# Exchanging the fourth sum over a and the fourth sum over b in the small round of a two-matmul kernel with GELU

## The chip, the cores and the metric

The kernel runs on one core of a Trainium2 chip. The metric is the device time of one execution in microseconds (us), and the time given for a kernel is the median of several runs. TensorE (PE in the profile; its weight loads are PEld) does the matrix products and writes them to PSUM, in eight banks of 128 x 512 fp32. VectorE (DVE) and ScalarE (ACT) read PSUM and the on-chip memory SBUF. GpSimd (POOL) and SyncE (SP) issue transfers here. Each engine works through its own list of instructions in the order in which the program gives them, and engines wait for each other by semaphores.

## The reference

```python
# a: 1024 x 1024, b: 1024 x 2048, c: 2048 x 1024, all float32
def reference(a, b, c):
    h = np.matmul(a, b)
    h = 0.5 * h * (1 + np.tanh(np.sqrt(2 / np.pi) * (h + 0.044715 * h ** 3)))
    return np.matmul(h, c).astype(np.float32)
```

Two matrix products with a GELU between them.

## The kernel before

The kernel holds the first product transposed: sixteen tiles of 128 columns of b, each against the 1024 rows of a, in two halves of 512. Tiles 0 to 3 are computed in the plain way while a and b are still coming in. Tiles 4 to 7 are the *small round*, tiles 8 to 15 the *large round*, and the product with c is a third one. Each round splits both of its operands into quarters and computes seven products of quarters where the plain way has eight; for this it needs sums and differences of quarters, which VectorE forms in SBUF. The sums over b are called s1 to s4 (`A` holds the quarters of b), the sums over a are t1 to t4 (`B` holds those of a).

```python
class Seven:
    def dve(self, dst, x, y, op, n=1, part=None):      # one sum, in n instructions
        w = self.kt // n
        for i in range(n) if part is None else (part,):
            r = slice(i * w, (i + 1) * w)
            nc.vector.tensor_tensor(out=dst[:, r], in0=x[:, r], in1=y[:, r], op=op)
    # ... cut: t1, t2, t3, s1, s2
    def t4(self, dst, n=1):
        self.last_t = dst
        self.dve(dst, self.t[1], self.B[1][0], SUB, n)
    def s3(self, n=1, part=None):
        self.dve(self.s[2], self.A[0][0], self.A[1][0], SUB, n, part)
    def s4(self, dst, n=1):
        self.last_s = dst
        self.dve(dst, self.A[0][1], self.s[1], SUB, n)
    # ... cut: plain_t, plain_s (copies on ScalarE)
    def product(self, p, l, r, j, start, c0=0, w=H):   # kt matmuls into one bank
        for k in range(self.kt):
            nc.tensor.matmul(p[:, ds(c0, w)], l[:, k, ts(j, 128)], r[:, k, ds(c0, w)],
                             start=(start and k == 0), stop=(k == self.kt - 1),
                             skip_group_check=not start)

BB = [[aT[:, 0, 0:4], aT[:, 1, 0:4]], [aT[:, 0, 4:8], aT[:, 1, 4:8]]]
zero = Seven(4, quarters(b1, H, 256), BB, [None] * 4, [None] * 4, 2)   # small round, n=2
one = Seven(4, quarters(b2, 0, H), BB, [None] * 4, zero.t)             # large round, n=4
```

In the small round `kt` is 4, so a product into one bank is four matmuls, and there are two banks (`n=2`): eight matmuls for each of the seven products. t4 is made by two instructions, each for two of the four k, and s4 by one.

```python
t4, x01 = pair(0)                      # halves of SBUF tiles x0, x1, x3
zero.s = [x31[:, :, 0:256], x01[:, :, 0:256], x11[:, :, 0:256], x01[:, :, 256:]]
one.s = [x31, x01, x11, x01]

def snap(tag, p, name):                # ScalarE copies a bank to SBUF
    st = pieces(tag, 4, [128, H], F32, name)
    nc.scalar.activation(st, p, AF.Copy)
    return st

def plus(p, st):                       # VectorE adds a bank and a copy
    ot = pieces("o", 4, [128, H], F32, "ot")
    nc.vector.tensor_tensor(out=ot, in0=p, in1=st, op=ADD)
    return ot

def seven(w, done, between):           # done applies the GELU (ScalarE) in the first two rounds
    # ... cut: names of the quarters and banks
    for j in J:
        w.product(px[j], A11, B11, j, True)                 # P1
        p1[j] = snap("m", px[j], "p1")                      # (a case of the third round is cut)
    between("P1")
    for j in J:
        p = bank(P2[j])
        w.product(p, A12, B21, j, True)                     # P2
        done(0, 0, j, plus(p, p1[j]))
    between("P2")
    py = [bank(i) for i in PY]
    for j in J:
        w.product(py[j], w.s[0], w.t[0], j, True)           # P5
    between("P5")
    for j in J:
        w.product(px[j], w.s[1], w.t[1], j, False)          # P6
        v[j] = snap("v", px[j], "v")
    between("P6")
    c22 = []
    for j in J:
        w.product(px[j], w.s[2], w.t[2], j, False)          # P7
        u[j] = snap("m", px[j], "u")
        c22.append(plus(py[j], u[j]))
        between(f"P7{j}")

    def p3(first):
        for j in J:
            if first:
                done(1, 1, j, c22[j])
            w.product(py[j], w.last_s, w.t[3], j, False)    # P3 reads s4
            done(0, 1, j, plus(py[j], v[j]))
        between("P3")

    def p4(first):
        for j in J:
            if first:
                done(1, 1, j, c22[j])
            w.product(px[j], w.s[3], w.last_t, j, False)    # P4 reads t4
            done(1, 0, j, px[j])

    for i, f in enumerate((p4, p3) if w.n == 2 else (p3, p4)):
        f(i == 0)
    # ... cut: the end of the third round

def between0(n):                       # VectorE's work between the products of the small round
    if n == "P1":
        zero.plain_s()
        zero.plain_t(2, 1)
    elif n == "P2":
        zero.s3()
        zero.s4(x31[:, :, 256:])
    elif n == "P5":
        zero.t4(t4, 2)
        one.last_t = t4

zero.s1()
zero.s2()
seven(zero, done0, between0)
one.s[3] = slot("b1", [128, 2, 4, H], F32R, "x1")[:, 0]
one.s1()
one.s2()
seven(one, done1, between1)
# ... cut: the third round, the product with c, and its stores
```

In the small round (`w.n == 2`) P4 runs ahead of P3; in the others P3 runs first. The large round uses the same t1 to t4 again.

Of the kernel before, what the change touches and what calls it, by code (L numbers as in the profile page):

```python
# [19 lines left out]
def kernel(ctx, tc, a, b, c, out):  # L20
# [183 lines left out]
    def quarters(b, c0, w):  # L204
        return [[b[:, 0:4, ds(c0, w)], b[:, 4:8, ds(c0, w)]],
                [b[:, 0:4, ds(c0 + w, w)], b[:, 4:8, ds(c0 + w, w)]]]

    zero = Seven(4, quarters(b1, H, 256), BB, [None] * 4, [None] * 4, 2)
# [151 lines left out]
    def between0(n):  # L360
        if n == "P1":
            zero.plain_s()
            zero.plain_t(2, 1)
        elif n == "P2":
            zero.s3()
            zero.s4(x31[:, :, 256:])
        elif n == "P5":
            zero.t4(t4, 2)
            one.last_t = t4

    def done1(i, l, j, p):
        gelu(8 + 4 * i + j, l, p)
# [16 lines left out]
# [5 lines that stand above are left out]
# [68 lines left out]
```

## Time and profile before

| | before |
|---|---|
| time, median of 3 runs | 120.03 us (119.86 to 120.13) |
| span of the profiled execution | 118.1 us |
| small round on TensorE | 26.0 to 39.4 us |
| large round on TensorE | 39.4 to 64.5 us |
| product with c on TensorE | 64.5 to 114.8 us |
| VectorE busy between 26.0 and 39.4 us | 10.85 of 13.40 us |
| ScalarE busy there | 10.13 us |
| TensorE's granted clock | 1.00 throughout |

A profile line such as `L152 DVE TENSOR_TENSOR x<-b,x` is an instruction of line 152 of the kernel (the sums are all in the helper `dve`, line 152; `plus` is line 283, `snap` 278, the GELU 107, and the matmuls of `product` 194), with the tile it writes and those it reads. What stands in square brackets behind it is the time its engine sat idle ahead of it, and what ended this wait. A matmul's end is modelled, while its start is recorded. The chain that ended last is followed back from the last instruction of the kernel, at each step to what released it.

### The profile page before, as it was taken

The page shows a single profiled execution, that of the slowest core. Times are in us where ns is not written, and L with a number is a line of the kernel's source. Part 1 is how long each engine was busy: PE and PEld are TensorE (multiplying, and loading weights), DVE is VectorE, ACT ScalarE, POOL GpSimd, SP SyncE. Part 2 cuts the span into 40 slices and gives each one's busy share as a digit, 9 for nine tenths or more (in the row PEclk, how much of TensorE's full clock was granted, in tenths as well). Part 3 has the DMA queues.
Part 4 walks back from the last instruction along what each step waited for, and adds up shares of the span by engine and source line. Part 5 has one row for each costly group of instructions (what it writes and reads, how often), then busy time and mean ns, then how long its engine had stood idle before and what let it go on. Part 6 is the DMA issues. An engine that isn't in the chain of part 4 may idle for free.

```text
span 118.1 us, 1469 instructions
## 1 busy us (share of the span) xinstructions
PE 111.9 (95%) x535; PEld 77.1 (65%) x540; DVE 90.5 (77%) x104; ACT 58.7 (50%) x96; POOL 11.0 (9%) x21
## 2 busy tenths in 40 slices
PE   5998899999998999999999999999999999999980
PEld 5654346544866545888887444588888888888860
DVE  0243697796996899772779999999999986964670
ACT  5046756899767689246679347800042992000000
POOL 2000007952223100000000000000000000000000
PEclk9999999999999999999999999999999999999999
DMA  3999999999999999999000000061000002014993
GB/s 88 289 371 366 366 354 305 177 205 207 205 206 213 211 212 212 211 211 212 15 0 0 0 6 0 0 221 45 0 0 0 0 0 92 3 39 175 364 350 137
DMA packets 13542, 17.91 MB, mean 152 GB/s; under 512 B 736, under 2 KB 8928, under 8 KB 13536
## 3 DMA queue, kind: packets, MB, share of 16 engines
q0 software_dynamic: 5344, 7.34, 35.2%
q1 hardware_dynamic: 8192, 10.49, 26.1%
q8 instruction: 4, 0.07, 0.2%
q14 instruction: 2, 0.02, 0.0%
HBM read 20.97 MB, written 4.19 MB: 213 GB/s over the span
## 4 chain that ended last, share of the span: by engine, by line
PE 80%; DMA 8%; DVE 5%; SPq 2%; issue 1%; ACT 1%; ACTq 0%; DVEq 0%
PE ps L194 69%; PE ps L103 8%; DMA sta<-in_a_dram 8%; DVE x L152 4%; PE pt L129 2%; SPq L68 1%; DVE ot L283 1%; ACT ab L97 1%; SPq L72 1%; DVE ot L349 0%; ACTq L97 0%; DVEq L283 0%
## 5 line engine op out<-in xcount | busy, mean ns | idle before, releaser
L194 PE MATMUL ps<-x,s 128*128 128x512 f32 x128 | 29.6, 391 | 0.0
L194 PEld LDWEIGHTS ps<-x,s 128*128 128x128 f32 x128 | 24.0, 188 | 5.1
L194 PE MATMUL ps<-x,x 128*128 128x512 f32 x96 | 22.9, 394 | 0.0
L194 PEld LDWEIGHTS ps<-x,x 128*128 128x128 f32 x96 | 18.0, 188 | 3.9
L103 PE MATMUL ps<-aT,b 128*128 128x512 bf16 x62 | 15.0, 379 | 0.7 <-DVE aT L131 0.5
L278 ACT ACTIVATE v<-ps 128x512 f32<-128x512 f32 x10 | 6.0, 598 | 17.8 <-PE ps L194 17.8
L194 PE MATMUL ps<-c_sb,hT 128*128 128x512 bf16 (+1 forms) x70 | 14.1, 355 | 0.1
L194 PE MATMUL ps<-x 128*128 128x512 f32 x56 | 13.5, 395 | 0.3 <-DVE x L152 0.3
L194 PEld LDWEIGHTS ps<-x 128*128 128x128 f32 x56 | 10.2, 188 | 3.3 <-DVE x L152 0.8
L107 ACT ACTIVATE hT<-ot 128x512 bf16<-128x512 f32 x18 | 10.7, 625 | 3.3 <-DVE ot L283 3.3
L283 DVE TENSOR_TENSOR ot<-ps,v 128x512 f32<-128x512 f32 x10 | 6.7, 687 | 6.4 <-DMA out_dram<-ot 3.9
L194 PEld LDWEIGHTS <-hT 128*128 128x128 bf16 x72 | 6.9, 98 | 7.0 <-issue 0.5
L194 PE MATMUL ps<-aT,b 128*128 128x512 bf16 x47 | 10.6, 379 | 0.1
L283 DVE TENSOR_TENSOR ot<-ps,u 128x512 f32<-128x512 f32 x10 | 6.7, 689 | 5.2 <-ACT u L278 5.2
L103 PEld LDWEIGHTS <-b 128*128 128x128 bf16 x64 | 5.8, 97 | 6.8 <-DVE aT L131 1.0
L131 DVE COPY aT<-pt 128x512 bf16<-128x512 bf16 x16 | 6.0, 419 | 5.2 <-PE pt L129 5.2
L152 DVE TENSOR_TENSOR x<-c_sb 128x1024 fp32r<-128x1024 bf16 x8 | 9.2, 1216 | 0.0
L194 PEld LDWEIGHTS <-b 128*128 128x128 bf16 x48 | 4.6, 98 | 5.7 <-issue 0.3
L152 DVE TENSOR_TENSOR x<-b 128x1024 fp32r<-128x1024 bf16 (+1 forms) x4 | 7.0, 1752 | 1.0 <-DMA b<-in_b_dram 1.0
L107 ACT ACTIVATE hT<-ps 128x512 bf16<-128x512 f32 x14 | 7.3, 596 | 0.5 <-PE ps L103 0.5
L278 ACT ACTIVATE u<-ps 128x512 f32<-128x512 f32 x10 | 5.8, 596 | 3.4 <-PE ps L194 3.2
L97 ACT ACTIVATE ab<-sta 128x512 bf16<-128x512 f32 (+1 forms) x7 | 5.0, 747 | 4.9 <-DMA sta<-in_a_dram 4.9
(39 smaller groups left out, 111.8 us busy)
## 6 DMA issues: line engine op xcount, KB each, us to landing
sta<-in_a_dram SPq DMA_DIRECT2D x8, 512.0 KB, 9.1
c_sb<-in_c_dram POOLq DMA_DIRECT2D x8, 512.0 KB, 19.8
b<-in_b_dram POOLq DMA_DIRECT2D x6, 512.0 KB, 10.9
out_dram<-ot SPq DMA_DIRECT2D x12, 256.0 KB, 2.1
stb<-in_b_dram SPq DMA_DIRECT2D x4, 512.0 KB, 8.7
out_dram<-ot SPq DMA_DIRECT2D x8, 128.0 KB, 2.0
```

Of the source, the lines that this page charges most:

```text
L68: nc.sync.dma_start(out=sta[q // 2][:, h, q % 2], in_=av[:, 4 * h:4 * h + 4, ds(q * 256, 256)])
L72: nc.sync.dma_start(out=stb[:, 2 * q:2 * q + 2], in_=bv[:, 2 * q:2 * q + 2, 0:H])
L97: nc.scalar.activation(dst, src, AF.Copy)
L103: nc.tensor.matmul(p, b1[:, k, ts(t, 128)], aT[:, h, k], start=(k == 0), stop=(k == KT - 1))
L107: nc.scalar.activation(hT[h][:, t], p, AF.Gelu_apprx_tanh)
L129: nc.tensor.transpose(pt[:, n, ts(m, 128)], ab[:, m, ts(n, 128)], ident)
L131: nc.vector.tensor_copy(aT[:, h, 2 * q + n], pt[:, n])
L152: nc.vector.tensor_tensor(out=dst[:, r], in0=x[:, r], in1=y[:, r], op=op)
L194: nc.tensor.matmul(p[:, ds(c0, w)], l[:, k, ts(j, 128)], r[:, k, ds(c0, w)], start=(start and k == 0), stop=(k == self.kt - 1), skip_group ...
L278: nc.scalar.activation(st, p, AF.Copy)
L283: nc.vector.tensor_tensor(out=ot, in0=p, in1=st, op=ADD)
```

## The change

In the small round, VectorE now forms t4 (the fourth sum over a) behind s3, and s4 (the fourth sum over b) behind t4; before, s4 came first. t4 is issued ahead of the product P5, s4 behind it. The point of it is the order in which the products ask for these sums: P4 reads t4, P3 reads s4, and in this round P4 comes first.

```diff
@@ -363,10 +363,10 @@
             zero.plain_t(2, 1)
         elif n == "P2":
             zero.s3()
-            zero.s4(x31[:, :, 256:])
-        elif n == "P5":
             zero.t4(t4, 2)
             one.last_t = t4
+        elif n == "P5":
+            zero.s4(x31[:, :, 256:])
 
     def done1(i, l, j, p):
         gelu(8 + 4 * i + j, l, p)
```

## Prediction

> **What bounds the kernel now.** I read the page first, then the chain that ended last over the small round, then the timeline of each engine there, then single starts.
>
> The page's first part and the first line of its part 4:
>
> ```profile
> PE 111.9 (95%) x535; PEld 77.1 (65%) x540; DVE 90.5 (77%) x104; ACT 58.7 (50%) x96; POOL 11.0 (9%) x21
> ...
> PE 80%; DMA 8%; DVE 5%; SPq 2%; issue 1%; ACT 1%; ACTq 0%; DVEq 0%
> ```
>
> TensorE (PE) is busy 95% of a 118.1 us span and carries 80% of the chain. VectorE (DVE) carries 5%, some 5.9 us. That piece is the interesting one, because the change is on VectorE. The chain between 29 and 42 us, in columns of start, length and what:
>
> ```profile
> 30.21 1.28 DVE ot L283 x2
> 31.49 4.55 DVE x L152 x4
> 36.04 0.04 issue
> 36.09 3.71 PE ps L194 x15
> ```
>
> So VectorE holds the end of the kernel for two additions of a bank and a copy (L283) and four sums (L152: s3, s4 and the two halves of t4). At 36.09 TensorE takes over, and from there to 114.81 the whole chain is TensorE with pieces of 0.05 us between; after 39.3 us its matmuls show no wait for another engine at all. The weight loads wait there three times 0.3 us, on "issue". Whatever moves 36.09 therefore moves the end by as much, unless something else stops TensorE on the way.
>
> VectorE's own timeline, from the sum s3 on (start, length, instruction):
>
> ```profile
> 31.41 1.22 DVE L152 TENSOR_TENSOR x<-b 128x1024 fp32r<-128x1024 bf16 x1
> 32.54 1.22 DVE L152 TENSOR_TENSOR x<-b,x 128x1024 fp32r<-128x1024 bf16 x1
> 33.67 2.36 DVE L152 TENSOR_TENSOR x<-x,aT 128x1024 fp32r<-128x1024 f32 x2
> 35.95 1.28 DVE L283 TENSOR_TENSOR ot<-ps,u 128x512 f32<-128x512 f32 x2
> 38.70 0.69 DVE L283 TENSOR_TENSOR ot<-ps,v 128x512 f32<-128x512 f32 x1 [1.47 <-PE ps L194]
> 39.60 0.69 DVE L283 TENSOR_TENSOR ot<-ps,v 128x512 f32<-128x512 f32 x1 [0.21 <-PE ps L194]
> ```
>
> They are s3, s4 (it reads b), t4 in two halves (it reads aT), the two additions that take c22 out of PSUM, then those that take the outputs of P3. No gap lies between the sums: their starts are 1.13 us apart. The same stretch on the weight loads and on the matmuls:
>
> ```profile
> 35.01 0.30 PEld L194 LDWEIGHTS ps<-x 128*128 128x128 f32 x2 [0.23 <-ACT u L278]
> 36.09 3.06 PEld L194 LDWEIGHTS ps<-x 128*128 128x128 f32 x14 [0.78 <-DVE x L152]
> ...
> 36.09 3.48 PE L194 MATMUL ps<-x 128*128 128x512 f32 x14 [0.34 <-DVE x L152]
> 39.41 3.84 PE L194 MATMUL ps<-aT,b 128*128 128x512 bf16 x16
> ```
>
> P4 and P3 are eight matmuls each. Two of P4's run at 35.01, then the loads stop for 0.78 us and 14 follow. So the stop is inside P4, ahead of its third matmul, k=2, the first that reads the second half of t4. That half starts at 34.81, takes 1.22 and ends at 36.03. P4 comes first of the two products in the small round, and needs t4; s4 is needed only by P3 behind it. VectorE makes them in the opposite order.
>
> **What the Trainium skill says.** "VectorE: DVE Perf Modes", The TRN2 errata, gives (N+151)/0.96 ns for a two-tensor add in fp32: 1224 ns for N=1024. The four sums here measure 1.22 us each, whichever input is bf16, so exchanging them costs nothing by itself. "PSUM — Partial Sum Buffer", Engine vs sequencer instructions, has VectorE's queue as strictly first in, first out, and matmuls in program order. The trace agrees: the last input of t4 (t2's second half, at 24.41 for 1.22 us) is ready at 25.63, yet t4 starts at 33.67, behind s4; and P3 does not overtake the stopped P4. "Perfetto Trace Analysis", Tensor Engine Instruction, warns that a matmul's end in a profile is an estimate. So I don't size the stop from the 0.34 us shown for PE, but from starts.
>
> **The change, part by part.** Nothing is added or removed, and the only difference in any engine's order of instructions is that VectorE's two halves of t4 stand ahead of s4. TensorE's program is the same. t4 gains no new wait; s4, which still waits only for VectorE itself, gains none for the product that reads the other half of its tile.
>
> 1. VectorE. s3 still starts at 31.41. t4's halves take the slots at 32.54 and 33.67 and end at 33.76 and 34.89. s4 takes the slot at 34.81 and ends at 36.03. The two c22 additions still start at 35.95 and end at 36.63 and 37.23. VectorE's work is 0 us shorter.
>
> 2. P4. Its first load waits for the ScalarE copy u of its bank, as now: u starts at 34.32, takes 0.60, and the load comes at 35.01. Single matmul starts of P4 in the trace: 35.06, 35.35, then 36.09, 36.43, 36.66 (the fifth is the first of the second bank). After a waited start the second matmul comes 0.29 later (35.06 to 35.35), and the others keep 0.23. Without the stop the third starts at 35.35 + 0.23 = 35.58, the fourth at 35.81, the fifth at 36.04. The gain at the third is 36.09 - 35.58 = 0.51 us. At the fifth it is 36.66 - 36.04 = 0.62, since the stop also costs a slow restart (0.34 instead of 0.23 behind 36.09).
>
> 3. The next limit on the fifth. It needs the second u copy, which starts at 35.25 and takes 0.60, so it ends at 35.85. From the first u, end 34.92 to load 35.01 is 0.09 us; that puts the load at 35.94. In the group before (v copy ends 33.94, load 33.99, matmul 34.13) the matmul followed its load by 0.13, so 36.07. That may take back 0.03 us. I keep a gain of about 0.6.
>
> 4. P3. Fifth at 36.04 to 36.07, plus four steps of 0.23: P3 starts at about 36.97. It needs s4 (36.03) and the bank that the first c22 addition reads (36.63); VectorE to TensorE took 0.06 (36.03 to 36.09). So 36.09 and 36.69: both early, the second by only 0.28. Its second bank starts near 37.9 and needs 37.23.
>
> 5. The large round. TensorE enters it at 39.41 now, at about 38.8 after. It needs bank 0 from the GELU that ends at 37.78, and bank 1 from the one that starts at 38.20 and takes 0.59: 38.79, while bank 1 is asked for four matmuls later, near 39.7. VectorE's additions of the P3 outputs wait for TensorE (1.47 and 0.21 us) and move with it, and so does the first sum of the large round, from 40.21 to 39.6. That sum needs the last piece of b; the issue of c that waits for it in the GpSimd queue goes out at 37.97, so it has come by then.
>
> 6. From there on no fixed time stands in the way that I can find. The loads of c end near 57 us (the page's GB/s line falls from 212 to 15 in slice 20), the first sum over c starts at 62.10, and TensorE's first use is at 64.49. Everything else hangs on TensorE or on VectorE, and both are 0.6 us earlier.
>
> The sum: 0 us of work, -0.62 us of wait, +0 to 0.03 of a new small wait: -0.6 us. 120.03 - 0.6 = 119.4 us, 0.5%.
>
> **The rivals.** One: another wait takes the place. For: at 0.03 to 0.3 us of slack, the second u copy and the first c22 addition are close behind t4. Against: they hang on TensorE and ScalarE work that doesn't get later. If the copy's wait costs a full 0.3, the time is 119.7. Two: the delay returns in P3, because s4 now ends at 36.03 and c22 behind it. P3 can't start before 36.69, against 37.59 now: even if it bound, 0.9 us would be gained at that point, so this cannot eat the gain, but a VectorE slower by half a microsecond in this stretch would; 119.9 then. Three: the large round swallows it (a bank, a piece of b), which gives 120.0. Against it are the 0.9 us of slack in bank 1 and 1.6 us on b. Four: more is gained than 0.6, because VectorE enters the long sums over c earlier; but TensorE has no wait there that could vanish. A loss would need s4 to be late for P3 by over a microsecond, and I see no reason.
>
> **Range and chances.** The three times before lie between 119.86 and 120.13, so a median of a few runs is good to about 0.15. With a gain between 0.3 and 0.8 that is 119.1 to 119.8. A 2% step would be 2.4 us, four times the whole stop, so faster by over 2% gets 1%, slower 1%, within 2% the rest.
>
> **What would show it.** Right: VectorE has t4 at 32.54 and 33.67 and s4 near 34.81; the 0.78 us of weight loads before 36.09 is gone, with at most 0.1 us for the second u in its place; the large round's first matmul is near 38.8; the chain no longer runs through VectorE at 36.09; the span is near 117.5. Wrong: P3's loads show a wait for L283 or L152 on VectorE; the large round starts near 39.4 in spite of an early P4; or s4 starts with a wait for TensorE.

## The result, and the profile after

| | before | after |
|---|---|---|
| time, median of 6 runs | 119.87 us (119.78 to 120.13) | 119.32 us (119.25 to 119.41) |
| ratio after to before, 95% interval | | 0.9951 (0.9938 to 0.9964) |
| span of the profiled execution | 118.1 us | 117.5 us |
| first matmul of P5 in the small round | 29.28 us | 29.40 us |
| first matmul of the large round | 39.40 us | 38.87 us |
| from the one to the other | 10.13 us | 9.47 us |

The change gains 0.55 us, or 0.5%, and the interval puts it at 0.4 to 0.7 us. The page after, the same two lines of its parts 1 and 4:

```profile
PE 110.8 (94%) x535; PEld 76.4 (65%) x540; DVE 90.5 (77%) x104; ACT 58.7 (50%) x96; POOL 11.0 (9%) x21
...
PE 85%; DMA 8%; SPq 2%; ACT 1%; issue 1%; DVE 0%; ACTq 0%
```

VectorE is as busy as before, 90.5 us, but has gone from 5% of the chain to 0%. The chain over the stretch from 29 to 42 us, which went through VectorE from 30.21 to 36.03 before, is TensorE alone now (start, length, what):

```profile
28.89 10.37 PE ps L194 x45
39.26 0.05 issue
39.31 2.75 PE ps L194 x12
```

VectorE's timeline from s3 on, after:

```profile
31.48 1.22 DVE L152 TENSOR_TENSOR x<-b 128x1024 fp32r<-128x1024 bf16 x1
32.61 2.35 DVE L152 TENSOR_TENSOR x<-x,aT 128x1024 fp32r<-128x1024 f32 x2
34.88 1.22 DVE L152 TENSOR_TENSOR x<-b,x 128x1024 fp32r<-128x1024 bf16 x1
36.02 1.28 DVE L283 TENSOR_TENSOR ot<-ps,u 128x512 f32<-128x512 f32 x2
38.16 0.69 DVE L283 TENSOR_TENSOR ot<-ps,v 128x512 f32<-128x512 f32 x1 [0.86 <-PE ps L194]
```

The order is s3, t4, s4; the c22 additions (L283 with u) come at the same place, 0.07 later only because the whole list of this execution is 0.07 later. Its wait for TensorE, ahead of the output of P3, has shrunk from 1.47 to 0.86 us. The weight loads and the matmuls after:

```profile
35.10 0.76 PEld L194 LDWEIGHTS ps<-x 128*128 128x128 f32 x4 [0.19 <-ACT u L278]
36.02 2.58 PEld L194 LDWEIGHTS ps<-x 128*128 128x128 f32 x12 [0.16 <-ACT u L278]
38.87 4.21 PEld L194 LDWEIGHTS <-b 128*128 128x128 bf16 x21 [0.26 <-issue]
...
33.26 5.77 PE L194 MATMUL ps<-x 128*128 128x512 f32 x24
38.87 4.49 PE L194 MATMUL ps<-aT,b 128*128 128x512 bf16 x19
```

The 0.78 us behind two loads of P4 is gone. The loads of P4's first bank now come as four in a row. Behind them the loads wait 0.16 us for the second u copy, and the other twelve of P4 and P3 follow. The 24 matmuls of P7, P4 and P3 are one piece without a gap.

### The profile page after: what moved, and what is told of

Same layout as the page of the kernel before. It is cut to its first block, busy times and chain, and to the rows that moved or that the text cites. A ratio compares the mean times of both kernels' runs of the same rounds, so it can differ in the third digit from the quotient of the medians.

```text
span 117.5 us, 1469 instructions
## 1 busy us (share of the span) xinstructions
PE 110.8 (94%) x535; PEld 76.4 (65%) x540; DVE 90.5 (77%) x104; ACT 58.7 (50%) x96; POOL 11.0 (9%) x21
## 4 chain that ended last, share of the span: by engine, by line
PE 85%; DMA 8%; SPq 2%; ACT 1%; issue 1%; DVE 0%; ACTq 0%
PE ps L194 75%; PE ps L103 8%; DMA sta<-in_a_dram 8%; PE pt L129 2%; SPq L68 1%; ACT ab L97 1%; SPq L72 1%; DVE ot L349 0%; ACTq L97 0%
## 5 line engine op out<-in xcount | busy, mean ns | idle before, releaser
L107 ACT ACTIVATE hT<-ot 128x512 bf16<-128x512 f32 x18 | 10.7, 626 | 2.6 <-DVE ot L283 2.6
L194 PEld LDWEIGHTS ps<-x 128*128 128x128 f32 x56 | 10.2, 188 | 2.6 <-ACT u L278 0.4
L283 DVE TENSOR_TENSOR ot<-ps,v 128x512 f32<-128x512 f32 x10 | 6.7, 688 | 5.7 <-DMA out_dram<-ot 3.9
L283 DVE TENSOR_TENSOR ot<-ps,u 128x512 f32<-128x512 f32 x10 | 6.7, 689 | 5.1 <-ACT u L278 5.1
L152 DVE TENSOR_TENSOR x<-c_sb 128x1024 fp32r<-128x1024 bf16 x8 | 9.3, 1220 | 0.0
L152 DVE TENSOR_TENSOR x<-b 128x1024 fp32r<-128x1024 bf16 (+1 forms) x4 | 7.0, 1751 | 1.0 <-DMA b<-in_b_dram 1.0
L107 ACT ACTIVATE hT<-ps 128x512 bf16<-128x512 f32 x14 | 7.3, 597 | 0.5 <-PE ps L103 0.5
```

Of the source, the lines that this page charges most:

```text
L107: nc.scalar.activation(hT[h][:, t], p, AF.Gelu_apprx_tanh)
```

## The experiments

Theory A is that of the prediction: the gain is TensorE's stop inside P4, on the second half of t4, and the next limit behind it is the first c22 addition, which must have read its bank before P3 adds onto it. The rivals are in the expectations. Two numbers are read from each run: the ratio to the kernel of before, timed beside it, and in its trace the stretch from the first matmul of P5 to the first of the large round (10.13 us before, 9.47 after). The stretch leaves out when P5 began; the last section tells why that is of use. Where VectorE is what TensorE waits for, the stretch also depends on how far ahead of P5 VectorE began s1, the first sum over b (1.47 us before, 1.52 after).

**Only the first half of t4 goes ahead of s4.** Against the changed kernel (`t4` is given the argument `part` of the other sums):

```diff
             zero.s3()
-            zero.t4(t4, 2)
-            one.last_t = t4
+            zero.t4(t4, 2, 0)
+            zero.s4(x31[:, :, 256:])
         elif n == "P5":
-            zero.s4(x31[:, :, 256:])
+            zero.t4(t4, 2, 1)
+            one.last_t = t4
```

> VectorE's order is s3, first half of t4, s4, second half of t4. Theory A (the gain is the stop of P4 at its third matmul, which waits for the second half of t4): that half ends near 36.1 us as before, the stop of about 0.65 us is back in full, 119.9 us, ratio 1.000 to before; the trace shows two matmuls of P4, then a wait for L152. Rival B (what counts is that t4 is begun earlier and s4 later): half or all of the gain stays, 119.3 to 119.6 us, ratio 0.995 to 0.998.

Measured: ratio 1.0022 (1.0001 to 1.0042), stretch 10.22 us. Its weight loads:

```profile
35.09 0.30 PEld L194 LDWEIGHTS ps<-x 128*128 128x128 f32 x2 [0.19 <-ACT u L278]
36.37 3.05 PEld L194 LDWEIGHTS ps<-x 128*128 128x128 f32 x14 [0.99 <-DVE x L152]
```

Two loads, then a wait for VectorE, as before. Nothing of the gain stays, so it hangs on when t4 is complete and not on when it is begun. Rival B falls. The ratio is a little above the 1.000 expected, so the run was repeated beside the kernel of before timed against itself, and the changed kernel.

> The order s3, first half of t4, s4, second half of t4, once more; it came out at 1.0022 where theory A wanted 1.000. Theory A (the excess is the scatter of the time at which b lands): ratio 1.000, within 0.002, and in the trace 10.1 to 10.2 us from the first matmul of P5 to the first of the large round, as before. Rival I (this order costs something of its own): 1.002 again, and a longer stretch than 10.2 us.

> The kernel of before, unchanged, timed against itself: what the comparison gives where there is no difference. Ratio 1.000, within 0.002. If it is off by 0.002 or more, differences of that size say nothing.

> The changed kernel once more, beside the other two on one chip: ratio 0.995, and 9.4 to 9.5 us from the first matmul of P5 to the first of the large round.

Measured: 1.0015 (0.9994 to 1.0036) with a stretch of 10.26 us; the kernel of before against itself 1.0008 (0.9984 to 1.0032) and 10.10 us; the changed kernel 0.9964 (0.9948 to 0.9981) and 9.44 us. The interval of the repeat holds 1.000, and its distance from before against itself is 0.0007. But the two stretches are 0.09 to 0.16 us over those of before (10.13 and 10.10), and 0.02 and 0.06 us over the 10.2 that was expected for no effect; there the result seems to lean to rival I. In both executions s1 began 1.37 us ahead of P5, against 1.47 and 1.51 us in the two of the kernel of before. The traces show where this comes from. The weight loads of P2 and the sum s1, in the profile of before and in that of `half_last`:

```profile
27.56 1.57 PEld L194 LDWEIGHTS <-b 128*128 128x128 bf16 x8 [0.15 <-DMA b<-in_b_dram]
27.81 1.23 DVE L152 TENSOR_TENSOR x<-b 128x1024 fp32r<-128x1024 bf16 x1 [1.03 <-DMA b<-in_b_dram]
...
27.85 1.41 PEld L194 LDWEIGHTS <-b 128*128 128x128 bf16 x8 [0.35 <-DMA b<-in_b_dram]
28.10 1.23 DVE L152 TENSOR_TENSOR x<-b 128x1024 fp32r<-128x1024 bf16 x1 [1.23 <-ACT p L278]
```

The loads wait for b, and s1 starts 0.25 us behind them in both (the last line names the copy p, which ended at 28.00 here; in the changed kernel with three idle sums, below, it ended at 27.98, and s1 still started 0.25 us behind the load, at 28.84). In every trace in which these loads wait 0.27 us or more, s1 begins 1.37 us ahead of P5. The repeat of the changed kernel is one of them (0.33 us), and so are four of the runs below. So the lead depends on when b lands, and not on the order of the sums. Counted from the start of s1, the large round begins 11.60 and 11.61 us later in the kernel of before, 11.59 in `half_last` and 11.63 in its repeat. That leaves at most 0.03 us for a cost of this order, and rival I falls too.

**P3 ahead of P4, the sums as before.** Against the kernel of before:

```diff
-        for i, f in enumerate((p4, p3) if w.n == 2 else (p3, p4)):
+        for i, f in enumerate((p3, p4)):
             f(i == 0)
```

> The sums stay in the order of before (s4, then t4), and P3 runs ahead of P4 in the small round, so that again each product finds its sum first in line. Theory A with its second limit (P3 adds onto the bank that the first c22 addition reads, and this stands behind all the sums and ends at 36.63): P3 can't start before 36.7 where P4 started at 35.06, TensorE stops 1.6 us instead of 0.65, so about 1.0 us slower than before: 120.9 us, ratio 1.008 (up to 1.010 if the large round then waits for the GELU that empties bank 0). Rival C (it is enough that sums and products stand in the same order, whichever it is): as after, 119.3 us, ratio 0.995.

Measured: ratio 1.0149 (1.0113 to 1.0185), some 1.8 us slower than before, where theory A wanted 1.0 to 1.2. Its VectorE, weight loads and matmuls (the profiled execution began the small round 1.3 us late, P5 at 30.61):

```profile
37.38 1.28 DVE L283 TENSOR_TENSOR ot<-ps,u 128x512 f32<-128x512 f32 x2
...
38.12 3.50 PEld L194 LDWEIGHTS ps<-x 128*128 128x128 f32 x16 [2.05 <-DVE ot L283]
...
42.28 1.02 PE L194 MATMUL ps<-aT,b 128*128 128x512 bf16 x4 [0.24 <-ACT hT L107]
```

The first stop is the one that theory A names: P3's first load comes 0.05 us behind the end of the first c22 addition (37.38 + 0.69 = 38.07) and waits for nothing else. Rival C falls: the same order in both lists is not enough, since the c22 additions stand behind all the sums in either case and P3, not P4, needs them. The size was off. The stretch is 11.67 us, 1.54 more than before. Of that, 0.10 is the shorter lead of s1 (1.37 us). Another 0.41 is a second stop, which I had given at most 0.2 us: the large round's first matmul started at 42.28 where P3 and P4 left room for it at 41.88. That leaves 1.03 us for the first stop, with 1.0 expected. The second stop waits for the GELU (L107) that empties bank 0, which is P4's own bank:

```profile
40.08 1.67 ACT L107 ACTIVATE hT<-ot 128x512 bf16<-128x512 f32 x3 [1.35 <-DVE ot L283]
41.66 1.06 ACT L107 ACTIVATE hT<-ps 128x512 bf16<-128x512 f32 x2
```

This GELU stands in ScalarE's list behind three others that come from VectorE, and starts at 41.66 without a gap behind them. By the profile the last matmul of P4 into its bank had ended at 41.13. Started then, with its 0.58 us, it would have been through at about 41.7 (an estimate), ahead of 41.88. So it was late by ScalarE's list, though with P4 last there is little room in any case. P4 first therefore has two reasons, of which the change uses one.

**s4 still further back, behind c22.** Against the changed kernel:

```diff
-        elif n == "P5":
+        elif n == "P71":
             zero.s4(x31[:, :, 256:])
```

> The changed kernel with s4 put further back, behind the two c22 additions. Theory A: c22 waits for the u copies (second at 35.97), ends near 36.70, s4 then ends at 37.84, while P3 wants it at 37.05: a new stop of 0.85 us and a slow restart of 0.1, so 120.2 to 120.3 us, ratio 1.003. The weight loads show the wait for L152 at the ninth of the sixteen loads of P4 and P3. Rival D (the further s4 goes back the better, because c22 and its GELU come earlier): 119.3 us or less, ratio 0.995 or less.

Measured: ratio 1.0037 (1.0019 to 1.0056), 120.25 us, stretch 10.41 us. Its weight loads:

```profile
34.87 0.77 PEld L194 LDWEIGHTS ps<-x 128*128 128x128 f32 x4 [0.19 <-ACT u L278]
35.79 0.78 PEld L194 LDWEIGHTS ps<-x 128*128 128x128 f32 x4 [0.16 <-ACT u L278]
37.64 1.67 PEld L194 LDWEIGHTS ps<-x 128*128 128x128 f32 x8 [1.07 <-DVE x L152]
```

As theory A has it: P4's eight loads are as in the changed kernel, and the ninth, P3's first, waits for s4. The stretch is 0.94 us longer than after, with 0.95 expected. Rival D falls: later is not better for s4, and of the places tried the one between t4 and c22 is good, the one behind c22 is not.

**t4's first half in the gap ahead of s1.** Against the changed kernel, with `part` as above:

```diff
             zero.s3()
-            zero.t4(t4, 2)
+            zero.t4(t4, 2, 1)
             one.last_t = t4
...
+    zero.t4(t4, 2, 0)
     zero.s1()
     zero.s2()
```

> The changed kernel with the first half of t4 made earlier still, in the 1 us in which VectorE waits for b ahead of s1; VectorE is then through with s4 and c22 about 1 us earlier. Theory A: nothing on TensorE waits for VectorE any more in the small round, so an earlier VectorE gains nothing: 119.3 us, ratio 0.995, as long as s1, at most 0.15 us later, still comes ahead of P5. Rival E (VectorE is still the bound of the small round, and the change gained only a part): up to another 0.5 us, 118.8 us, ratio 0.991.

Measured: ratio 0.9954 (0.9937 to 0.9972), 119.32 us, stretch 9.40 us. VectorE and the matmuls:

```profile
33.78 1.22 DVE L152 TENSOR_TENSOR x<-b,x 128x1024 fp32r<-128x1024 bf16 x1
34.92 0.69 DVE L283 TENSOR_TENSOR ot<-ps,u 128x512 f32<-128x512 f32 x1
35.81 0.69 DVE L283 TENSOR_TENSOR ot<-ps,u 128x512 f32<-128x512 f32 x1 [0.20 <-ACT u L278]
...
33.08 5.77 PE L194 MATMUL ps<-x 128*128 128x512 f32 x24
```

s4 is made 1.1 us earlier and the first c22 addition 1.1 us earlier, and the 24 matmuls take 5.77 us as in the changed kernel. The stretch is 0.07 us shorter, but 0.06 of that lies in P5 itself, whose second matmul came 0.36 us behind the first instead of 0.42; the repeat of the changed kernel shows the same (0.35). An earlier VectorE gains nothing now: the change took all that this stop had to give. Rival E falls.

**A push of measured size on VectorE, ahead of s4, in both kernels.** One or three idle sums of 256 columns, whose results are not used; against the changed kernel, and likewise ahead of `zero.s4` in the kernel of before:

```diff
+    def idle(m):
+        for _ in range(m):
+            junk = pieces("e", 2, [128, 256], F32, "junk")
+            nc.vector.tensor_tensor(out=junk, in0=warm, in1=warm, op=ADD)
...
+            idle(3)
             zero.s4(x31[:, :, 256:])
```

> The kernel of before with one idle sum of 256 columns on VectorE ahead of s4 (its result is not used). It should take about 0.42 us and push what follows back by some 0.33. Theory A (before, t4 has no slack against P4): the end moves by the whole push, +0.33 us, 120.2 us, ratio 1.003. Rival F (TensorE bounds the kernel, VectorE's list has slack): ratio 1.000.

> The kernel of before with three such sums ahead of s4, a push of about 1.0 us. Theory A: no slack, the end moves by the whole push, 120.9 us, ratio 1.0085. With after_plus3 it shows that the gain of the change is capped by the slack of c22: between these two kernels it should be 0.9 to 1.0 us less the 0.7 to 0.8 that after_plus3 loses, added to the 0.6 of the change, so about 0.85 us. Rival F: ratio below 1.004.

> The changed kernel with the same idle sum ahead of s4. Theory A: s4 has 0.9 us of slack to P3; the first c22 addition behind it ends at 36.70, P3 needs it at about 37.0, so 0.3 us of slack, against a push of 0.33: 0 to 0.1 us slower than the changed kernel, 119.3 to 119.4 us, ratio 0.995 to 0.996. Rival G (the gain was only moved to s4, which now has no slack): +0.33, ratio 0.998.

> The changed kernel with three such sums, a push of about 1.0 us. Theory A: c22 then ends near 37.7 and P3, wanted at 37.05, starts near 37.8: 0.7 us lost and up to 0.1 of slow restart, so 120.0 to 120.1 us, ratio 1.001 to 1.002; the loads of P3 wait for L283, not for L152 (s4 ends at 37.1, its wait is 0.1 at most). Rival H (s4 is the next limit and c22 has slack): 119.4 us, ratio 0.996. Rival G: ratio 1.0035.

| idle sums (push) | before: ratio | before: stretch | after: ratio | after: stretch |
|---|---|---|---|---|
| none | 1 | 10.13 us | 0.9951 (0.9938 to 0.9964) | 9.47 us |
| one (0.33 us) | 1.0028 (1.0010 to 1.0046) | 10.55 us | 0.9949 (0.9931 to 0.9967) | 9.67 us |
| three (1.00 us) | 1.0095 (1.0064 to 1.0125) | 11.20 us | 1.0019 (0.9999 to 1.0039) | 10.47 us |

The push is read from VectorE's starts: in the changed kernel with one sum, 34.77 to 35.10, and with three, 35.85 to 36.85. Before, the whole push reaches the end: 0.0028 and 0.0095 of 120 us are 0.34 and 1.14 us. The stretches grow by 0.43 and 1.07 us; s1's lead was 0.10 and 0.08 us shorter in these two executions, which leaves 0.33 and 0.99, the push itself. VectorE's list had no slack against P4, and rival F falls. After, the first push is not seen in the time, and the second is. The weight loads of the changed kernel with one sum, where P3 begins:

```profile
36.98 1.69 PEld L194 LDWEIGHTS ps<-x 128*128 128x128 f32 x8 [0.33 <-DVE ot L283]
```

and with three:

```profile
38.72 1.69 PEld L194 LDWEIGHTS ps<-x 128*128 128x128 f32 x8 [1.20 <-DVE ot L283]
```

P3 waits for L283, the c22 addition, and not for L152, the sum s4: rivals G and H fall, and the next limit is where the prediction had it, about 0.3 us away. The size was again a little low: in the stretch, one sum costs 0.20 us against the 0 to 0.1 expected. P3's eight matmuls up to the large round take 1.96 us behind this short wait (36.98 to 38.94) and 1.82 in the changed kernel (37.05 to 38.87). So some 0.14 us of the 0.20 is the slow restart, and the wait itself is 0.06. In the time this does not show, but its interval is 0.2 us either way. The run with three sums had a late small round in its profile (P5 at 30.21), with VectorE's s1 0.15 us later against P5 than in the changed kernel. Of the 1.00 us that its stretch grew this leaves 0.84; the time grew by 0.0068 of 120, 0.8 us, as expected. Between the two kernels with three sums lie 0.0076 of 120, or 0.9 us, where 0.85 was expected.

## Why the prediction was right

1. **VectorE.** Right: t4 at 32.61, s4 at 34.88 and c22 at 36.02 are the predicted starts plus the 0.07 by which this execution's list lies later. Nothing became longer or shorter.

2. **P4.** Right. Its first five matmuls started at 35.17, 35.44, 35.67, 35.90 and 36.14. From first to fifth that is 0.96 us, against 1.61 before: a gain of 0.65 where 0.62 was worked out. The 0.34 us that the profile shows as idle for TensorE before would have been half of it. Working from starts was the right choice.

3. **The second u copy.** The wait appeared, 0.16 us in the loads where at most 0.1 was given, and cost 0.01 at most: the fifth matmul came 0.24 behind the fourth, as the fourth did behind the third within 0.01. The copy ended at 35.97 and the load came at 36.02, so the hand-over took 0.05 and not the 0.09 I had used.

4. **P3.** It started at 37.05 (predicted 36.97, plus 0.1 for the later execution), with c22 ended at 36.70 and s4 at 36.10. The slack of c22, 0.28 worked out, is shown by the two runs with idle sums: 0.33 us of push is nearly free, 1.00 costs 0.8.

5. **The large round.** It began at 38.87, predicted 38.8. No bank or piece of b held it up.

6. **The rest.** From the large round's first matmul to the kernel's last one it took 75.12 us before and 75.12 after. All that was gained ahead of it arrived.

The sum was -0.6 us. In the pair of profiles the stretch shrank by 0.66, and P5 began 0.12 later by chance, so the span shrank by 0.54. The times gave 0.55, and the repeat 0.0036 of 120, or 0.43 (interval 0.23 to 0.62). Of the rivals of the prediction the first came nearest, in the second u copy's wait of 0.16 us, which TensorE's spacing covered. The second, P3 as the new limit, had to be brought about by a push on VectorE; the third and the fourth did not occur.

Two of its sums about the way to a loss were wrong, and the result did not depend on them. A VectorE slower by half a microsecond was to eat the gain (119.9). With the prediction's own slack of 0.28 for c22 it would take 0.22 of the 0.6; the pushes took nothing that the time shows for 0.33 us, and 0.8 for 1.00. And a loss was to need an s4 late for P3 by over a microsecond. With s4 behind c22, P3 started 0.82 us later against P5 than in the changed kernel, and this was already slower than before (1.0037).

What else the prediction didn't see is small: the slow restart, which it counted in P4 as part of the gain but left out of the next limit, and the second reason for P4 to be first.

## What to carry to other kernels

Where an engine works through a list in order, put what is wanted first at the front, and ask for the time at which each piece is complete: exchanging two items of equal cost moved the end by the full stop. Before moving an item, follow what stands behind it too, since s4 and c22 kept their deadlines here only by 0.9 and 0.3 us, and one place further back cost 0.9 us. And size a stop of TensorE from the starts of its matmuls, with the restart, not from the idle time shown beside them.

## What the runs showed that I had not expected

In all thirteen traces, of ten different kernels and on more than one chip, the stretch from the first matmul of the large round to the last of the kernel is 75.12 us to within 0.01. All that differs between executions of one kernel lies ahead of that, and most of it ahead of P5, whose first matmul came anywhere from 29.17 to 30.61 us. The latest is that of the run with P3 first: in its chain the transfer of a takes 10.44 us, where it takes 9.11 before, and all behind it is 1.3 us later. The profiled execution with three idle sums took 121.11 us where the median was 120.19, and its weight loads show why (the pieces of b for P1 and P2):

```profile
26.06 1.42 PEld L194 LDWEIGHTS <-b 128*128 128x128 bf16 x8 [0.31 <-DMA b<-in_b_dram]
28.60 1.41 PEld L194 LDWEIGHTS <-b 128*128 128x128 bf16 x8 [1.12 <-DMA b<-in_b_dram]
```

They waited 1.43 us for b there, and 0.15 in the profile of before; from the first matmul of P1 to that of P5 it took 4.12 us instead of 3.27. A difference of a few tenths between two profiles of this kernel is therefore first of all a matter of when a and b landed. A stretch that begins behind them can tell an effect of 0.1 us: repeated, it differed by 0.03 us for either kernel (10.13 and 10.10, 9.47 and 9.44). The times, 119.1 to 121.2 us for the kernel of before alone, leave 0.2 us either way with 22 executions of the one kernel beside more than 50 of the other. The stretch from P5 is not quite free of b either, as s1's lead shows: where TensorE waits for VectorE, the start of s1 is the better place to count from.

A stop of TensorE costs more than its wait. Behind a wait for another engine the second matmul came 0.34 us after the first (36.09 to 36.43, before; the same in the runs where P3 waited for c22 or s4), where 0.23 is the usual spacing, and P3 behind a wait of 0.06 us took 0.14 us longer.
